# Two heads at a time: alternating the halves of the TensorE array in a block's attention matmuls

## The chip, the cores and the metric

The kernel runs on one core of a Trainium2 chip. The time is device microseconds of one execution, and the figure compared is the median of several executions.

## The reference

Two transformer blocks run one after the other on 256 tokens of width 1024, all in float32. Only the first block's attention matters here. It has two kinds of heads, eight each, of width 64, over 272 positions (16 meta tokens and the input):

```python
# forgetting attention, blocks of queries
s = einsum('bhqd,bhkd->bhqk', q, k) * scale
s = s + c[:, :, start:end, None] - c[:, :, None, :end]      # c = cumsum(log f)
p = softmax(where(s_pos <= t_pos, s, -inf))
out = einsum('bhqk,bhkd->bhqd', p, v)

# stick-breaking attention
z = einsum('bhqd,bhkd->bhqk', q, k) * scale
log_keep = where(s_pos < t_pos, log_sigmoid(-z), 0)
later = cumsum(log_keep, reverse=True) - log_keep
a = where(s_pos < t_pos, exp(log_sigmoid(z) + later), 0)
out = einsum('bhqk,bhkd->bhqd', a, v)
```

The second block has, among other things, a differential attention whose eight heads each have two score matrices of width 64.

## The kernel before

**The stream of projections.** Weights come in slabs (1024 rows by 256 columns as a rule) over SyncE's queue. ScalarE rounds each half slab to a high part (L87), and VectorE subtracts it from the raw weights to give the low part (L96). TensorE multiplies tile by tile: a tile is 128 output features, eight blocks of the contraction, three matmuls each (high by high, low by high, high by low; L320, L321, L323), 24 matmuls of 258 or 272 columns. After each tile comes one call of `period`: it starts a weight split, advances the evacuations of the last tiles, advances the side tasks by one stage, and finishes the weight split. `Side.tick` takes a new task from its queue when the clock, which counts these calls, has reached a due time; the task's gap sets the next due time. So side work is written into each engine's queue between two tiles, and the order is fixed when the kernel is written.

**Attention as side tasks.** A head's query and key are features by tokens, with head h in rows 0 to 63 or 64 to 127 of chunk h // 2. `ev_q` scales the query chunk and queues two tasks, one for each head: `fox` (forgetting) with a gap of 2 calls, `sbk` (stick-breaking) with a gap of 1.5.

- `scores` (L669 to L674) takes a PSUM bank, writes the additive causal mask into it with a bfloat16 matmul by the identity (418 columns), and adds the scores of three key blocks with float32 matmuls on the head's 64 rows: 258, 144 and 16 columns.
- `fox`: the second stage takes the maximum over key blocks (L685 and the helper at L308) and an all-reduce over partitions on GpSimd (L689). Two calls later three VectorE operations and an exponential (L696) give e. The next stage multiplies by `vext` (L699 to L703), values in 64 columns and ones in the other 64, so that numerators and denominators come in one product. Then ScalarE copies both (L710, L711), and after the odd head VectorE divides (L714) and splits the result.
- `sbk`: the second stage computes the softplus on ScalarE (L724 to L726), VectorE and ScalarE again (high part at L311, low part at L312). The third adds the reversed cumulative sum with triangular matrices (L735). The fourth takes an exponential (L738) and multiplies by the values (L743, L745, L747): 64 columns of weights, all 128 rows, and the output goes to rows 0 to 63 of a bank for the even head and 64 to 127 for the odd one. After the odd head the result is split.

A float32 matmul shows as two instructions in the trace. Score and value banks, and the banks of transposed value chunks (`ev_v`, L621 to L633), come from one pool `at` of four banks; projections have four banks of their own.

**A like pattern elsewhere.** The second block's `diff` (L1156) loops over two query blocks and, inside, over the two row halves c of the same chunk, with the outputs in two banks.

Of the kernel before, what the change touches and what calls it, by code (L numbers as in the profile page):

```python
# [11 lines left out]
F32R = mybir.dt.float32r  # L12
BF16 = mybir.dt.bfloat16
AF = mybir.ActivationFunctionType
ALU = mybir.AluOpType
# [3 lines left out]
P = 128  # L19
# [30 lines left out]
class Weights:  # L50
    """Streams weight slabs: DMA, then an exact split into two float32r parts."""

# [68 lines left out]
class Side:  # L121
    """Advances evacuations and queued side tasks by one stage per call."""

# [46 lines left out]
def two_blocks_kernel(  # L170
# [64 lines left out]

# [1 line left out]
    tab = cp.tile([P, 256], F32, name="tab")  # L237
# [52 lines left out]

# [1 line left out]
    def bank(pool, tag):  # L292
        return pool.tile([P, 512], F32, tag=tag, name=tag)

    def at():
        return bank(atp, "at")
# [4 lines left out]
    def mul(o, a, b):  # L301
        V.tensor_tensor(o, a, b, ALU.mult)  # L302
# [4 lines left out]
    def stt(o, a, s, b, op0=ALU.mult, op1=ALU.mult):  # L307
        V.scalar_tensor_tensor(out=o, in0=a, scalar=s, in1=b, op0=op0, op1=op1)  # L308
# [65 lines left out]
    class Sums:  # L374
        """Sums of squares over features, with tokens on the partitions."""

# [41 lines left out]
    def tp_tile(tag, n):  # L418
        if tag == "acc":
            return tp.tile([P, NQ], F32, tag="acc", name="acc", bufs=2)[:, :n]  # L420
        if n <= L1:
            return tp.tile([P, L1], F32, tag="s", name=tag, bufs=8)[:, :n]
        return tp.tile([P, 418], F32, tag="b", name=tag, bufs=7)[:, :n]
# [79 lines left out]

# [1 line left out]
    R = cp.tile([P, KD, NQ], F32, name="R")  # L505
# [101 lines left out]

# [1 line left out]
    u4 = unit("u4", shape=(P, KD, L1))  # L609
# [50 lines left out]
    def ev_q(q, task, gap):  # L660
        def go(ps, c):
            mul(q[:, c, :], ps[:, :NQ], rb8)
            side.add(task(2 * c), gap)
            side.add(task(2 * c + 1), gap)
            yield
        return go

    def scores(S, m, k, q, c, r):
        T.matmul(S[:, 0:418], identb, maskb[:, m, :], start=True, stop=False, skip_group_check=True)  # L669
        k, q = k[r:r + 64, c, :], q[r:r + 64, c, :]  # L670
        T.matmul(S[:, 0:258], k[:, 0:128], q, start=False, stop=False, skip_group_check=True)  # L671
        T.matmul(S[:, 258:402], k[:, 128:256], q[:, 114:258], start=False, stop=False,
                 skip_group_check=True)
        T.matmul(S[0:16, 402:418], k[:, 256:272], q[:, 242:258], start=False, stop=True,  # L674
                 skip_group_check=True)

    pair = {}

    def fox(h):
        c, r = h // 2, 64 * (h % 2)  # L680
        S = at()
        scores(S, 0, ka, qa, c, r)
        yield
        m = tp_tile("m", NQ)
        V.tensor_scalar(out=m, in0=S[:, 0:258], scalar1=ccol[:, 0, h:h + 1], scalar2=None, op0=ALU.add)  # L685
        stt(m[:, 114:258], S[:, 258:402], ccol[:, 1, h:h + 1], m[:, 114:258], ALU.add, ALU.max)
        stt(m[:, 242:258], S[:, 402:418], ccol[:, 2, h:h + 1], m[:, 242:258], ALU.add, ALU.max)
        mx = tp_tile("mx", NQ)
        G.partition_all_reduce(mx, m, P, bass_isa.ReduceOp.max)  # L689
        yield  # L690
        yield
        e = tp_tile("e", 418)
        stt(e[:, 0:258], S[:, 0:258], ccol[:, 0, h:h + 1], mx, ALU.add, ALU.subtract)
        stt(e[:, 258:402], S[:, 258:402], ccol[:, 1, h:h + 1], mx[:, 114:258], ALU.add, ALU.subtract)
        stt(e[:, 402:418], S[:, 402:418], ccol[:, 2, h:h + 1], mx[:, 242:258], ALU.add, ALU.subtract)
        A.activation(e, e, AF.Exp)  # L696
        yield
        ps = at()
        T.matmul(ps[:, 0:258], vext[:, 0, h, :], e[:, 0:258], start=True, stop=False,  # L699
                 skip_group_check=True)  # L700
        T.matmul(ps[:, 114:258], vext[:, 1, h, :], e[:, 258:402], start=False, stop=False,
                 skip_group_check=True)
        T.matmul(ps[:, 242:258], vext2[:, h, :], e[0:16, 402:418], start=False, stop=True,  # L703
                 skip_group_check=True)
        yield
        if r == 0:
            pair["o"] = tp_tile("po", NQ)
            pair["d"] = tp_tile("pd", NQ)
        po, pd = pair["o"], pair["d"]
        A.activation(po[r:r + 64], ps[r:r + 64, :NQ], AF.Copy)  # L710
        A.activation(pd[r:r + 64], ps[64 - r:128 - r, :NQ], AF.Copy)  # L711
        if r:
            yield
            V.reciprocal(pd, pd)  # L714
            mul(po, po, pd)
            split(Oh[:, c, :], Ol[:, c, :], po)

    def sbk(h):
        c, r = h // 2, 64 * (h % 2)
        S = at()  # L720
        scores(S, 1, kb, qb, c, r)
        yield
        a = tp_tile("e", 418)
        A.activation(a, S[:, 0:418], AF.Abs)  # L724
        A.activation(a, a, AF.Exp, scale=-1.0)
        A.activation(a, a, AF.Ln, bias=1.0)  # L726
        stt(a, S[:, 0:418], 0.0, a, ALU.max, ALU.add)
        ah, al = [tp.tile([P, 418], F32R, tag="b", name="sp", bufs=7) for _ in range(2)]
        split(ah, al, a)
        yield  # L730
        for o, l, i in ((S[:, 0:418], trir, ah), (S[:, 0:418], trir, al),
                        (S[:, 114:258], nones, a[:, 258:402]),
                        (S[:, 128:416].rearrange("p (a c) -> p a c", a=2)[:, :, 114:130], nones,
                         a[:, None, 402:418].to_broadcast([P, 2, 16]))):
            T.matmul(o, l, i, start=False, stop=True, skip_group_check=True)  # L735
        yield
        e = tp_tile("p", 418)
        A.activation(e, S[:, 0:418], AF.Exp)  # L738
        if r == 0:
            pair["s"] = at()  # L740
        ps = pair["s"]
        hs = slice(h * 64, h * 64 + 64)
        T.matmul(ps[r:r + 64, 0:258], vb[:, 0, hs], e[:, 0:258], start=True, stop=False,  # L743
                 skip_group_check=True)
        T.matmul(ps[r:r + 64, 114:258], vb[:, 1, hs], e[:, 258:402], start=False, stop=False,  # L745
                 skip_group_check=True)
        T.matmul(ps[r:r + 64, 242:258], vb2[:, hs], e[0:16, 402:418], start=False, stop=True,  # L747
                 skip_group_check=True)
        if r:
            yield  # L750
            split(Oh[:, 4 + c, :], Ol[:, 4 + c, :], ps[:, 0:258])

# [40 lines left out]
    for i in (0, 2):  # L793
        linear(feat_tiles(1, X1, 0, L1), KD, at_offset(ev_k(ka), i))
        linear(feat_tiles(1, X1, T0, NQ), KD, at_offset(ev_q(qa, fox, 2.0), i))
    linear(feat_tiles(2, X1, 0, L1), KD, ev_k(kb))
    linear(feat_tiles(2, X1, T0, NQ), KD, ev_q(qb, sbk, 1.5))
    linear(feat_tiles(2, X1, 0, L1), KD, lambda ps, c: ev_v(ps, c, False))
# [20 lines left out]

# [1 line left out]
    def ev_fox(ps, j):  # L821
# [54 lines left out]
    def residual(sums, after, toks, off, n, gout, gnext, fill):  # L876
        """The next linear's input from a normed residual: a maker of one chunk at a time."""
        side.evac()
# [54 lines left out]
    def ple_filler(W, stages):  # L933
        """Spreads the embedding's products over a residual's waits: one bank at a time."""
        held = []

        def fill(stage):
            if stage == 3:
                dst, src = held.pop(0)
                A.activation(dst, src, AF.Copy)  # L940
                return
            for t, c in stages[stage]:
                ps = at() if len(held) < 3 else mm()
                ts, cs = slice(t * P, (t + 1) * P), slice(c, c + 512)
                for k in range(2):
                    mm3(ps, ph[:, k, ts], pl[:, k, ts], W[0][:, k, cs], W[1][:, k, cs], k == 0, k == 1)
                held.append((ple[:, t, cs], ps))
        return fill

    box = {}  # L950

# [1 line left out]
    s1 = Sums(TOKQ, acc=True, mixed=True)  # L953
# [76 lines left out]

# [1 line left out]
    hi = unit("xh", F32R, (P, KD, L1))  # L1032
# [289 lines left out]

# [1 line left out]
    def ev_brd(ps, j):  # L1324
# [44 lines left out]

# [1 line left out]
    gh = [unit(f"u{i}", F32R) for i in (0, 1, 2, 4)]  # L1371
# [37 lines left out]

# [1 line left out]
    gfin = unit("u0", shape=(P, D))  # L1411
# [90 lines left out]
```

## Time and profile before

| | |
|---|---|
| median of 3 runs | 951.78 us (950.01 to 952.24) |
| span of the profiled execution | 950.2 us (the page gives no time around it) |
| TensorE busy | 923.9 us, 97% of the span |
| VectorE busy | 648.3 us, 68% |
| ScalarE busy | 523.5 us, 55% |
| GpSimd busy | 91.5 us, 10% |
| chain that ended last | TensorE 79%, VectorE 15%, issue 2%, ScalarE 2%, DMA 1% |

The span goes from the first to the last instruction of one execution. Busy times of one engine are the union of its instructions. Matmuls are pipelined, so their durations overlap; what one costs is read from its start to the next start.

### The profile page before, as it was taken

The numbers are of one execution on the slowest core, as the hardware profiler recorded it, in microseconds if no ns is written. First come the engines' busy times: TensorE is split into PE (matmuls) and PEld (weight loads), VectorE is DVE, ScalarE is ACT, GpSimd is POOL, SyncE is SP. The second block draws the span as 40 slices with busy tenths as digits, with TensorE's granted clock in tenths as the row PEclk, the third lists the DMA queues.
The fourth block names the chain that finished last, engine by engine and source line by source line (L and its number), as shares of the span: only waits on it lengthen the run. The fifth ranks groups of instructions, "written<-read, shape, count | busy, mean of one in ns | idle before, by whom it ended". The sixth has DMA issues, their size and how long they took to land.

```text
span 950.2 us, 18312 instructions
## 1 busy us (share of the span) xinstructions
PE 923.9 (97%) x7457; PEld 894.6 (94%) x7457; DVE 648.3 (68%) x1150; ACT 523.5 (55%) x948; POOL 91.5 (10%) x75
## 2 busy tenths in 40 slices
PE   7999999999999999899899999999999999999996
PEld 5999988999899999899899999999999999999996
DVE  4667664577699999734767774577787666655546
ACT  5534565466576666545656665445555565544435
POOL 4022100022332222001300000000000000000000
PEclk7999999999999999899999999999999999999998
DMA  8554434456255565565265556455475566565531
GB/s 263 156 156 122 121 90 111 133 180 210 89 156 178 178 179 178 167 208 179 90 202 157 152 170 192 139 165 170 136 225 173 177 200 185 177 209 179 187 130 45
DMA packets 149715, 154.73 MB, mean 163 GB/s; under 512 B 5260, under 2 KB 145808, under 8 KB 149632
## 3 DMA queue, kind: packets, MB, share of 16 engines
q1 hardware_dynamic: 147904, 149.56, 52.4%
q0 software_dynamic: 1376, 3.36, 1.1%
q8 instruction: 58, 0.95, 0.4%
q10 hardware_dynamic: 352, 0.66, 0.2%
q14 instruction: 25, 0.20, 0.1%
HBM read 152.50 MB, written 1.05 MB: 162 GB/s over the span
## 4 chain that ended last, share of the span: by engine, by line
PE 79%; DVE 15%; issue 2%; ACT 2%; DMA 1%; POOL 0%; SPq 0%; DVEq 0%; ACTq 0%
PE mm L320 20%; PE mm L323 19%; PE mm L321 19%; DVE cv L308 5%; DVE wlo L96 4%; PE mm L336 4%; PE mm L334 4%; PE mm L333 4%; DVE ur L302 2%; PE at L671 1%; DVE cv L302 1%; DMA raw<-in_w_in_dram 1%; PE at L735 1%; PE at L1156 1%; DVE u L981 1%
## 5 line engine op out<-in xcount | busy, mean ns | idle before, releaser
L87 ACT ACTIVATE whi<-raw 128x1024 fp32r<-128x1024 f32 (+1 forms) x284 | 292.3, 1047 | 186.5 <-PE mm L323 90.9
L96 DVE TENSOR_TENSOR wlo<-raw,whi 128x1024 fp32r<-128x1024 f32 (+1 forms) x267 | 325.0, 1225 | 100.1 <-ACT whi L87 99.8
L323 PE MATMUL mm<-xl,whi 128*128 128x258 f32 (+2 forms) x1256 | 351.4, 283 | 1.3 <-DVE xl L308 1.3
L320 PE MATMUL mm<-xh,whi 128*128 128x258 f32 (+3 forms) x1192 | 342.8, 288 | 3.4 <-ACT xh L542 3.4
L321 PE MATMUL mm<-xh,wlo 128*128 128x258 f32 (+3 forms) x1192 | 337.5, 284 | 0.3 <-DVE wlo L96 0.3
L323 PEld LDWEIGHTS mm<-xl,whi 128*128 128x128 f32 x1256 | 235.8, 189 | 2.0 <-DVE xl L308 1.7
L320 PEld LDWEIGHTS mm<-xh,whi 128*128 128x128 f32 (+1 forms) x1192 | 225.1, 189 | 7.0 <-ACT xh L542 3.4
L321 PEld LDWEIGHTS mm<-xh,wlo 128*128 128x128 f32 (+1 forms) x1192 | 225.2, 189 | 1.6 <-DVE wlo L96 1.2
L320 PE MATMUL mm<-u,whi 128*128 128x256 f32 (+1 forms) x704 | 198.4, 282 | 0.0
L321 PE MATMUL mm<-u,wlo 128*128 128x256 f32 (+1 forms) x704 | 197.1, 280 | 0.0
L323 PE MATMUL mm<-u,whi 128*128 128x256 f32 (+1 forms) x576 | 162.6, 282 | 0.0
L321 PEld LDWEIGHTS mm<-u,wlo 128*128 128x128 f32 x704 | 133.1, 189 | 0.0
L320 PEld LDWEIGHTS mm<-u,whi 128*128 128x128 f32 x704 | 132.5, 188 | 0.0
L323 PEld LDWEIGHTS mm<-u,whi 128*128 128x128 f32 x576 | 108.4, 188 | 0.0
L333 PE MATMUL mm<-whi,u 128*128 128x256 f32 x240 | 68.7, 286 | 2.4 <-ACT whi L87 2.4
L334 PE MATMUL mm<-wlo,u 128*128 128x256 f32 x240 | 68.9, 287 | 1.5 <-DVE wlo L96 0.9
L336 PE MATMUL mm<-whi,u 128*128 128x256 f32 x240 | 68.6, 286 | 0.0
L308 DVE SCALAR_TENSOR_TENSOR cv<-ur,gc,cv 128x256 f32<-128x256 f32 x88 | 66.3, 756 | 1.6
L96 POOL TENSOR_TENSOR wlo<-raw,whi 128x1024 fp32r<-128x1024 f32 x17 | 40.8, 2405 | 176.1 <-ACT whi L87 94.2
L302 DVE TENSOR_TENSOR u<-mm,rb 128x256 f32<-128x256 f32 (+2 forms) x68 | 28.9, 425 | 40.1 <-PE mm L323 40.1
L333 PEld LDWEIGHTS mm<-whi,u 128*128 128x128 f32 x240 | 46.4, 193 | 2.6 <-ACT whi L87 2.6
L334 PEld LDWEIGHTS mm<-wlo,u 128*128 128x128 f32 x240 | 46.6, 194 | 1.9 <-DVE wlo L96 1.1
(343 smaller groups left out, 1088.4 us busy)
## 6 DMA issues: line engine op xcount, KB each, us to landing
raw<-in_w_in_dram SPq DMA_DIRECT2D x102, 512.0 KB, 3.8
raw<-in_w_ff_dram SPq DMA_DIRECT2D x64, 512.0 KB, 3.9
raw<-in_w_up_dram SPq DMA_DIRECT2D x44, 512.0 KB, 3.6
raw<-in_w_out_dram SPq DMA_DIRECT2D x16, 512.0 KB, 4.4
raw<-in_w_down_dram SPq DMA_DIRECT2D x16, 512.0 KB, 4.8
raw<-in_w_branch_diff_dram SPq DMA_DIRECT2D x8, 512.0 KB, 3.5
raw<-in_w_branch_ret_dram SPq DMA_DIRECT2D x8, 512.0 KB, 3.4
raw<-in_w_ple_gate_dram SPq DMA_DIRECT2D x8, 512.0 KB, 3.8
```

Source lines behind the costliest of these rows:

```text
L87: self.nc.scalar.activation(hi[:, a:b], w, AF.Copy)
L96: eng.tensor_tensor(lo, w, f32(hi), ALU.subtract)
L302: V.tensor_tensor(o, a, b, ALU.mult)
L308: V.scalar_tensor_tensor(out=o, in0=a, scalar=s, in1=b, op0=op0, op1=op1)
L320: T.matmul(ps, sh, mh, start=first, stop=False)
L321: T.matmul(ps, sl, mh, start=False, stop=False)
L323: T.matmul(ps, sh, ml, start=False, stop=last)
L333: T.matmul(ps[:, 0:256], hi, W[0][:, k, :], start=first, stop=False)
L334: T.matmul(ps[:, 0:256], hi, W[1][:, k, :], start=False, stop=False)
L336: T.matmul(ps[:, 0:256], lo, W[0][:, k, :], start=False, stop=last)
L671: T.matmul(S[:, 0:258], k[:, 0:128], q, start=False, stop=False, skip_group_check=True)
L735: T.matmul(o, l, i, start=False, stop=True, skip_group_check=True)
```

## The change

The side tasks take a chunk (two heads) instead of a head. `scores` writes two masks, and then alternates the rows for each key block. `sbk` multiplies the values of both heads in alternation, into the two row halves of one bank. The gaps are doubled. The work of the other engines is written for both heads in one stage. Lines that only repeat the old stages for two heads are left out here.

```diff
     def ev_q(q, task, gap):
         def go(ps, c):
             mul(q[:, c, :], ps[:, :NQ], rb8)
-            side.add(task(2 * c), gap)
-            side.add(task(2 * c + 1), gap)
+            side.add(task(c), gap)
             yield
...
-    def scores(S, m, k, q, c, r):
-        T.matmul(S[:, 0:418], identb, maskb[:, m, :], start=True, stop=False, skip_group_check=True)
-        k, q = k[r:r + 64, c, :], q[r:r + 64, c, :]
-        T.matmul(S[:, 0:258], k[:, 0:128], q, start=False, stop=False, skip_group_check=True)
-        T.matmul(S[:, 258:402], k[:, 128:256], q[:, 114:258], start=False, stop=False,
-                 skip_group_check=True)
-        T.matmul(S[0:16, 402:418], k[:, 256:272], q[:, 242:258], start=False, stop=True,
-                 skip_group_check=True)
+    ROWS = (slice(0, 64), slice(64, 128))
+    def scores(S, m, k, q, c):
+        for i in range(2):
+            T.matmul(S[i][:, 0:418], identb, maskb[:, m, :], start=True, stop=False,
+                     skip_group_check=True)
+        for o, kk, qq in ((slice(0, 258), slice(0, 128), slice(0, 258)),
+                          (slice(258, 402), slice(128, 256), slice(114, 258)),
+                          (slice(402, 418), slice(256, 272), slice(242, 258))):
+            for i, r in enumerate(ROWS):
+                T.matmul(S[i][0:kk.stop - kk.start, o], k[r, c, kk], q[r, c, qq], start=False,
+                         stop=kk.stop == 272, skip_group_check=True)
...
+    def sbk(c):
+        S = [at(), at()]
+        scores(S, 1, kb, qb, c)
+        yield
+        parts = []
+        for s in S:
+            a = tp_tile("e", 418)
+            A.activation(a, s[:, 0:418], AF.Abs)
+            A.activation(a, a, AF.Exp, scale=-1.0)
+            A.activation(a, a, AF.Ln, bias=1.0)
+            stt(a, s[:, 0:418], 0.0, a, ALU.max, ALU.add)
+            ah, al = [tp.tile([P, 418], F32R, tag="b", name="sp", bufs=7) for _ in range(2)]
+            split(ah, al, a)
+            parts.append((a, ah, al))
+        yield
...
+        es = [tp_tile("p", 418) for _ in S]
+        for e, s in zip(es, S):
+            A.activation(e, s[:, 0:418], AF.Exp)
         ps = at()
...
+        for o, v, x, first in ((slice(0, 258), lambda hs: vb[:, 0, hs], lambda e: e[:, 0:258], True),
+                               (slice(114, 258), lambda hs: vb[:, 1, hs], lambda e: e[:, 258:402], False),
+                               (slice(242, 258), lambda hs: vb2[:, hs], lambda e: e[0:16, 402:418], False)):
+            for i, r in enumerate(ROWS):
+                h = 2 * c + i
+                T.matmul(ps[r, o], v(slice(h * 64, h * 64 + 64)), x(es[i]), start=first,
+                         stop=o.start == 242, skip_group_check=True)
...
-        linear(feat_tiles(1, X1, T0, NQ), KD, at_offset(ev_q(qa, fox, 2.0), i))
+        linear(feat_tiles(1, X1, T0, NQ), KD, at_offset(ev_q(qa, fox, 4.0), i))
...
-    linear(feat_tiles(2, X1, T0, NQ), KD, ev_q(qb, sbk, 1.5))
+    linear(feat_tiles(2, X1, T0, NQ), KD, ev_q(qb, sbk, 3.0))
```

## Rows read from the trace of the kernel before

**Rows 1.** The page: TensorE's busy time, and its granted clock in 40 slices.
```profile
PE 923.9 (97%) x7457; PEld 894.6 (94%) x7457; DVE 648.3 (68%) x1150; ACT 523.5 (55%) x948; POOL 91.5 (10%) x75
...
PEclk7999999999999999899999999999999999999998
```

**Rows 2.** Windows view: stretch, busy us by engine, PEclk, DMA share, GB/s.
```profile
47.80:181.00 133.20, 133.20 (x965) 120.09 (x963) 80.51 (x139) 65.75 (x109) 15.31 (x8) 1.00 0.44 122
385.00:405.00 20.00, 16.74 (x116) 16.34 (x115) 12.04 (x16) 12.06 (x19) 0.00 (x0) 0.83 0.58 189
```

**Rows 3.** Instructions of L671 and of L743: durations, first and last start, forms.
```profile
L671 PE MATMUL at<-u x32: 377/430/483, 48.1 to 167.7; 64*128 64x258 f32 x32
...
L743 PE MATMUL at<-p,u x16: 380/407/433, 129.0 to 180.4; 128*64 128x258 f32 x16
```

**Rows 4.** Timeline of TensorE, scores of one stick-breaking head: start, us, instruction.
```profile
161.73 0.34 PE L669 MATMUL at<-maskb,identb 128*128 128x418 bf16 x1
162.00 0.70 PE L671 MATMUL at<-u 64*128 64x258 f32 x2
...
162.87 0.21 PE L674 MATMUL at<-u 64*16 64x16 f32 x2
163.01 0.39 PE L320 MATMUL mm<-xh,whi 128*128 128x258 f32 x1
163.23 0.28 PE L321 MATMUL mm<-xh,wlo 128*128 128x258 f32 x1
163.35 0.28 PE L323 MATMUL mm<-xl,whi 128*128 128x258 f32 x1
```

**Rows 5.** Windows view of L1156 alone: stretch, TensorE busy (instructions in flight), PEclk.
```profile
500.50:500.53 0.03, 0.01 (x2) 1.00 0.19 68
```

**Rows 6.** Timeline of TensorE, second block, scores of one differential head.
```profile
500.52 0.93 PE L1156 MATMUL at<-u,u 64*128 64x128 f32 x8
501.37 0.39 PE L320 MATMUL mm<-xh,whi 128*128 128x256 f32 x1
```

**Rows 7.** Timeline of TensorE, values of one stick-breaking head.
```profile
159.82 0.65 PE L743 MATMUL at<-p,u 128*64 128x258 f32 x2
...
160.86 0.65 PE L735 MATMUL at<-sp,trir 128*128 128x418 f32 x2
```

**Rows 8.** Timeline of TensorE, vext matmuls of one forgetting head.
```profile
113.77 0.60 PE L699 MATMUL at<-e,u 128*128 128x258 f32 x2
...
114.86 0.35 PE L669 MATMUL at<-maskb,identb 128*128 128x418 bf16 x1
```

**Rows 9.** Timeline of VectorE, forgetting heads.
```profile
77.05 1.75 DVE L714 RECIPROCAL pd<-pd 128x258 f32<-128x258 f32 x1
...
80.16 1.22 DVE L96 TENSOR_TENSOR wlo<-raw,whi 128x1024 fp32r<-128x1024 f32 x1
...
81.64 0.90 DVE L308 SCALAR_TENSOR_TENSOR e<-at,ccol,mx 128x258 f32<-128x258 f32 x3
82.45 0.48 DVE L685 TENSOR_SCALAR m<-at,ccol 128x258 f32<-128x258 f32 x1
...
83.53 1.21 DVE L96 TENSOR_TENSOR wlo<-raw,whi 128x1024 fp32r<-128x1024 f32 x1
```

**Rows 10.** Timeline of ScalarE, one stick-breaking head's softplus.
```profile
163.12 0.52 ACT L724 ACTIVATE e<-at 128x418 f32<-128x418 f32 x1 [0.67 <-PE at L674]
163.67 0.56 ACT L725 ACTIVATE e<-e 128x418 f32<-128x418 f32 x1
...
165.47 0.55 ACT L311 ACTIVATE sp<-e 128x418 fp32r<-128x418 f32 x1 [0.66 <-DVE e L308]
166.17 1.06 ACT L87 ACTIVATE whi<-raw 128x1024 fp32r<-128x1024 f32 x1
```

**Rows 11.** Groups by line, 20 to 320 us: GpSimd's all-reduces (busy us, mean ns).
```profile
L689 POOL PARTITION_ALL_REDUCE mx<-m x8 | 15.3, 1913 | 79.4 <-DVE m L308 79.4
```

**Rows 12.** Timeline of VectorE, the same head's low part.
```profile
166.06 0.60 DVE L312 TENSOR_TENSOR sp<-e,sp 128x418 fp32r<-128x418 f32 x1 [0.62 <-ACT sp L311]
```

More of the change, by code (lines that the diff above doesn't have):

```diff
@@ L677, in two_blocks_kernel @@
[L677 to L682, printed above, removed]
-        yield
[L684 to L689, printed above, removed]
+    ROWS = (slice(0, 64), slice(64, 128))
@@ new lines, in fox @@
+    def fox(c):
+        heads = (2 * c, 2 * c + 1)
+        S = [at(), at()]
+        scores(S, 0, ka, qa, c)
+        yield
+        mx = []
+        for i, h in enumerate(heads):
+            m = tp_tile("m", NQ)
+            V.tensor_scalar(out=m, in0=S[i][:, 0:258], scalar1=ccol[:, 0, h:h + 1], scalar2=None,
+                            op0=ALU.add)
+            stt(m[:, 114:258], S[i][:, 258:402], ccol[:, 1, h:h + 1], m[:, 114:258], ALU.add, ALU.max)
+            stt(m[:, 242:258], S[i][:, 402:418], ccol[:, 2, h:h + 1], m[:, 242:258], ALU.add, ALU.max)
+            mx.append(tp_tile("mx", NQ))
+            G.partition_all_reduce(mx[i], m, P, bass_isa.ReduceOp.max)
@@ L690, in fox @@
         yield
         yield
[L692 to L696, printed above, removed]
-        yield
-        ps = at()
-        T.matmul(ps[:, 0:258], vext[:, 0, h, :], e[:, 0:258], start=True, stop=False,
-                 skip_group_check=True)
@@ L701, in fox @@
[L701 to L704, printed above, removed]
-        yield
[L706 to L751, printed above, removed]
@@ new lines, in fox @@
+        es = []
+        for i, h in enumerate(heads):
+            e = tp_tile("e", 418)
+            for k, (o, n) in enumerate(((0, 258), (258, 144), (402, 16))):
+                stt(e[:, o:o + n], S[i][:, o:o + n], ccol[:, k, h:h + 1], mx[i][:, 258 - n:258],
+                    ALU.add, ALU.subtract)
+            A.activation(e, e, AF.Exp)
+            es.append(e)
+        yield
+        ps = [at(), at()]
+        for i, h in enumerate(heads):
+            e = es[i]
+            T.matmul(ps[i][:, 0:258], vext[:, 0, h, :], e[:, 0:258], start=True, stop=False,
+                     skip_group_check=True)
+            T.matmul(ps[i][:, 114:258], vext[:, 1, h, :], e[:, 258:402], start=False, stop=False,
+                     skip_group_check=True)
+            T.matmul(ps[i][:, 242:258], vext2[:, h, :], e[0:16, 402:418], start=False, stop=True,
+                     skip_group_check=True)
@@ new lines, in fox @@
+        yield
+        po, pd = tp_tile("po", NQ), tp_tile("pd", NQ)
+        for i, r in enumerate(ROWS):
+            A.activation(po[r], ps[i][r, :NQ], AF.Copy)
+            A.activation(pd[r], ps[i][ROWS[1 - i], :NQ], AF.Copy)
+        yield
+        V.reciprocal(pd, pd)
+        mul(po, po, pd)
+        split(Oh[:, c, :], Ol[:, c, :], po)
+    def sbk(c):
+        S = [at(), at()]
+        scores(S, 1, kb, qb, c)
+        yield
+        parts = []
[8 more added lines that the diff above has]
+            parts.append((a, ah, al))
+        yield
+        for s, (a, ah, al) in zip(S, parts):
+            for o, l, i in ((s[:, 0:418], trir, ah), (s[:, 0:418], trir, al),
+                            (s[:, 114:258], nones, a[:, 258:402]),
+                            (s[:, 128:416].rearrange("p (a c) -> p a c", a=2)[:, :, 114:130], nones,
+                             a[:, None, 402:418].to_broadcast([P, 2, 16]))):
+                T.matmul(o, l, i, start=False, stop=True, skip_group_check=True)
+        yield
+        es = [tp_tile("p", 418) for _ in S]
+        for e, s in zip(es, S):
+            A.activation(e, s[:, 0:418], AF.Exp)
+        ps = at()
+        for o, v, x, first in ((slice(0, 258), lambda hs: vb[:, 0, hs], lambda e: e[:, 0:258], True),
+                               (slice(114, 258), lambda hs: vb[:, 1, hs], lambda e: e[:, 258:402], False),
+                               (slice(242, 258), lambda hs: vb2[:, hs], lambda e: e[0:16, 402:418], False)):
+            for i, r in enumerate(ROWS):
+                h = 2 * c + i
+                T.matmul(ps[r, o], v(slice(h * 64, h * 64 + 64)), x(es[i]), start=first,
+                         stop=o.start == 242, skip_group_check=True)
+        yield
+        split(Oh[:, 4 + c, :], Ol[:, 4 + c, :], ps[:, 0:258])
```

## The prediction

> **What bounds the kernel now.** I read the page first: TensorE is busy 97% of the span, and its granted clock is full in nearly all of the 40 slices [rows 1]. The windows view says the same of the stretch of the first block's attention: from 47.8 to 181.0 us TensorE is busy 133.20 of 133.20 us at a clock of 1.00, VectorE 80.5 and ScalarE 65.8 us [rows 2]. So in this stretch what TensorE spends is what the kernel spends, and the other engines matter only if they make it wait. The count of the two lines that the change regroups says how often they come: 32 half-matmuls of L671 between 48.1 and 167.7 us (16 heads, two instructions for each float32 matmul) and 16 of L743 (8 heads) [rows 3]. I then read start to start in the order of time, because the busy times of pipelined matmuls overlap.
>
> **Scores, before.** One head's scores run from the mask matmul at 161.73 to the next projection matmul at 163.01: 1.28 us, of which 0.27 goes from the mask's start to the first 64-row matmul (418 columns at the pace of the projections, 258 in 0.12, would be 0.19; the rest is the change from 128 rows to 64) and 1.01 to the six half-matmuls on 64 rows [rows 4]. The first projection matmul after them takes 0.22 to the next start where a later one takes 0.12: 0.10 for going back [rows 4]. So a head costs 1.28 + 0.10 = 1.38 us, sixteen heads 22.1 us.
>
> **Scores, after.** A pair issues two masks, then 258, 144 and 16 columns, each for rows 0 to 63 and at once for rows 64 to 127, into two different banks. Does this overlap? The second block's differential attention already does it: L1156 issues 128 and 256 columns for two row halves into two banks. In a window of 0.03 us around 500.52 two of its matmuls have started [rows 5], and its eight halves take 0.85 us (500.52 to 501.37) [rows 6]: that is two heads in the time in which here one head's 258 and 144 columns take 0.87 (162.00 to 162.87) [rows 4]. So I take the second half as free. A pair then costs 0.19 (first mask) + 1.28 + 0.10 = 1.57 us against 2.76: 1.19 less, **9.5 us** over eight pairs. Bounds: a second mask that costs the full 0.27 takes back 0.08 x 8 = 0.6; no overlap at all leaves only the saved changes of rows, 0.27 - 0.19 + 0.10 = 0.18 a pair, 1.4 us.
>
> **Stick-breaking values.** One head's value matmuls (L743, L745, L747; 64 columns of weights, all rows) run from 159.82 to 160.86: 1.04 us, eight heads 8.3 us [rows 7]. After, the halves alternate between column halves 0 to 63 and 64 to 127 of one bank, each with its own 128-row moving operand. No row here shows two column halves in flight together. Bounds: full overlap gives 4 x 1.04 = 4.2 us; one after the other gives 0; if each of the five hand-overs in a pair costs the 0.10 that a change of rows costs, 2.0 us are lost. I take 4.2, because the nearest row is the other kind of half on the same array, and that overlaps within 0.03 us.
> The Trainium skill, on the page "TensorE: Matmul & The Clock Gate", section "Packing small matmuls — row/col tiling", says that a weight load overlaps matmuls in flight only when the row group differs; column halves share all row groups. By that rule the value term would be 0 and the sum 9.5 instead of 13.7. No run here shows column halves side by side; the same section also lists a speedup for column tiles.
>
> **What stays beside.** The vext matmuls of the forgetting heads (1.09 us a head, 113.77 to 114.86 [rows 8]) and the triangular ones are the same instructions, now two heads at one call, and I cost them at nothing. ScalarE, VectorE and GpSimd do the same operations, but two heads in one call of the side queue, every four (forgetting) or three (stick-breaking) calls instead of two or one and a half. So the question is whether TensorE now waits.
> Forgetting heads: in four calls TensorE has four tiles of 24 matmuls at 0.12 = 11.5, two heads' vext matmuls 2.2 and a pair's scores 1.5: 15.2 us. VectorE has four times a product and a low split (1.48), one reciprocal group (77.05 to 80.16, 3.11), two times e (0.81) and two times m (1.08) [rows 9]: 12.8 us. In order: m can start when the scores are done, 3.8 us after the call; both m end at 6.0; split and product 7.4; the previous pair's reciprocal group 10.6; split and product 12.0; e of the first head 12.9, of the second 13.7. With an exponential of 0.56 [rows 10] the values are ready at 13.4 and 14.2, and TensorE asks for them at 15.2 and 16.3. Hidden, by 1.8 us. The two all-reduces of 1.9 us on GpSimd [rows 11] run one behind the other from 4.9 to 8.7, before e needs them; nothing else stands in that queue.
> Stick-breaking heads: one head's chain goes from the absolute value at 163.12 to the end of the high split at 166.02 on ScalarE [rows 10] and to 166.66 on VectorE [rows 12]. The second head follows on ScalarE 2.90 later, so the last low part is ready 2.90 + 3.54 = 6.4 us after the scores. TensorE comes back after two tiles, 5.8 us, works 0.9 us on the first head's triangular matmuls (160.86 to 161.73 [rows 4, 7]), and wants the second head's low part at about 6.8. Hidden, by 0.4 us only. What is queued behind on ScalarE is the weight split of the following call (1.06 us [rows 10]), whose slab TensorE needs about two tiles later.
> Banks: at one call the last forgetting pair holds two, a transposed value chunk one, and the first stick-breaking pair asks for two, five of a pool of four. The last waits for ScalarE's two copies of the chunk, behind one split of 1.06; 2.2 us of vext matmuls cover it. Uncovered it would cost some 2 us, once. SyncE's weight loads keep their order and follow TensorE; no DMA is added or moved.
>
> **Sum.** 9.5 + 4.2 = 13.7 us. The profiled execution's span is 950.2, so its own span would be 936.5. The page gives no time around the span; the runs (950.01 to 952.24) leave under 2 us for it, and their median 951.78 stands 1.6 above the span. Against the median: 951.8 - 13.7 = **938.1**.
>
> **Rivals.**
> *Only the row halves overlap* (scores gain, values don't). For: no row shows column halves together, and two full 128-row operands would have to stream at once, which the row halves don't ask for. Against: nothing in the rows either. 951.8 - 9.5 = 942.3, up to 944.3 with the hand-overs. The rule of the Trainium skill cited above would make it this case.
> *The pair's chain is late.* For: the stick-breaking margin is 0.4 us; one weight split on ScalarE (1.06) and its low part on VectorE (1.22 [rows 9]) between the two heads make TensorE wait 1.9 us in each of four pairs: 938.1 + 7.5 = 945.6. Against: the splits are issued ahead of the pair in each call, and ScalarE reaches them while TensorE still does the scores.
> *Slower than before.* The same wait at L735, with two splits and two low parts in the chain (4.6 us): 4.2 x 4 = 16.7 us, 954.8. It decides from 13.7 / 4 = 3.4 us of wait a pair, a chain of 10.2 instead of 6.4 us. VectorE's and ScalarE's shares of 60% and 50% [rows 2] speak against it.
> *It doesn't do what it says*: the score halves don't overlap, say because they add to a bank that the mask has just filled, which L1156 does not. Then 1.4 us are left: 950.4.
>
> **How the numbers follow.** Forecast 0.55, only rows 0.26, late chain 0.12, no overlap 0.04, slower 0.03. About 0.3%, 2.9 us, is what a measurement of this kernel can tell from no change. Faster by more than that: the first three, 0.93; within it: 0.04; slower: 0.03. The range 934.5 to 944.3 holds the first two cases with their bounds, 0.81. Its lower end also has the clock: from 385 to 405 us the granted clock is 0.83 [rows 2], so 6.8 of 20 us run at 1.2 GHz instead of 2.4, after TensorE was idle 3.3 us in that window; everything there comes some 14 us earlier, and if the slow piece doesn't come, half of it, 3.4 us, is gained.
>
> **What would show it.** Right: the row halves start in pairs some 0.01 us apart; a pair's scores take about 1.5 us from the first mask to the next projection matmul; L743 to L747 take 1.04 us for two heads; TensorE has no idle time in the stretch, which ends 13 to 14 us earlier. Wrong: 2.1 us for a pair's values (then 942.3); TensorE idle in front of L735 or L699, released by ScalarE or VectorE (late chain); scores of 2.6 us a pair (no overlap).

## The result, and the profile after

| | before | after |
|---|---|---|
| median | 951.92 us (950.01 to 952.24, 4 runs) | 937.26 us (936.75 to 937.62, 4 runs) |
| span of the profiled execution | 950.2 us | 935.8 us |
| first mask matmul to first output projection | 142.1 us | 129.7 us |

The ratio is 0.9848, with a 95% interval of 0.9836 to 0.986: 1.5% faster. The forecast was 938.1. In the runs shown here an execution's time is some 1.8 us above its span (937.62 for the profiled one, with a span of 935.8), which the page of the kernel before did not tell.

The page after, the rows that answer to [rows 1]:
```profile
PE 909.7 (97%) x7457; PEld 884.8 (95%) x7457; DVE 647.0 (69%) x1150; ACT 522.5 (56%) x948; POOL 88.1 (9%) x75
...
PEclk8999999999999999999999999999999999999998
```
TensorE runs the same 7457 matmuls and is busy 14.2 us less; the other engines have what they had. (GpSimd's 3.4 us less is in its all-reduces, which now come two at a time: the trace shows the first of a pair as 1.1 us instead of 1.9.)

For the stretch itself I take two points that both kernels have: the first mask matmul, and the first matmul of the output projections behind the attention. The windows view of that stretch, first of the kernel before and then of the changed one (stretch, busy us by engine in the order PE, PEld, DVE, ACT, POOL, then the clock):
```profile
47.83:189.91 142.08, 142.08 (x1039) 128.97 (x1037) 85.27 (x144) 70.06 (x114) 15.31 (x8) 1.00 0.44 123
```
```profile
45.97:175.64 129.67, 128.59 (x1038) 119.79 (x1037) 84.66 (x144) 69.11 (x114) 11.93 (x8) 1.00 0.46 134
```
The stretch is 12.4 us shorter at a full clock. Before, TensorE was never idle in it; now it is for 1.08 us. The span fell by 14.4: 12.4 here, and 1.9 because the stretch begins at 45.97 and not at 47.83, though nothing ahead of it was changed. That part is told apart below.

One call of the side queue after, in the timeline of TensorE; the rows that answer to [rows 4] and [rows 7], now for two heads:
```profile
136.68 0.28 PE L323 MATMUL mm<-xl,whi 128*128 128x258 f32 x1
136.89 0.90 PE L756 MATMUL at<-p,u 128*64 128x258 f32 x8
137.73 0.29 PE L756 MATMUL at<-p,ple 16*64 16x16 f32 x4
137.95 0.53 PE L672 MATMUL at<-maskb,identb 128*128 128x418 bf16 x2
138.41 1.10 PE L678 MATMUL at<-u 64*128 64x258 f32 x12
139.44 0.39 PE L320 MATMUL mm<-xh,whi 128*128 128x258 f32 x1
139.66 0.28 PE L321 MATMUL mm<-xh,wlo 128*128 128x258 f32 x1
```
Values of two heads: 136.89 to 137.95, 1.06 us, where one head took 1.04. Scores of two heads with both masks: 137.95 to 139.44, 1.49 us, where one head took 1.28. The windows view of L678 (row halves) and of L756 (column halves), cut to 0.03 us around a start, has two matmuls in flight in each case. The last line is the same view of the column halves in the run of the first experiment below, which has one half after the other and shows one:
```profile
138.40:138.43 0.03, 0.02 (x2) 1.00 0.86 307
...
136.88:136.91 0.03, 0.02 (x2) 1.00 0.64 205
...
136.45:136.48 0.03, 0.02 (x1) 1.00 0.45 137
```
So the two in flight are the two halves, and both kinds run side by side. And the one idle piece, in the view of who waited for whom (engine and line waited for: us, times, longest):
```profile
PE at L756 <- ACT p L749: 1.1, 1, 1.1
```

### The profile page after: what moved, and what is told of

Its sections match the earlier page's. It is cut to its first block, busy times and chain, and to the rows that moved or that the text cites. A ratio compares the mean times of both kernels' runs of the same rounds, so it can differ in the third digit from the quotient of the medians.

```text
span 935.8 us, 18318 instructions
## 1 busy us (share of the span) xinstructions
PE 909.7 (97%) x7457; PEld 884.8 (95%) x7457; DVE 647.0 (69%) x1150; ACT 522.5 (56%) x948; POOL 88.1 (9%) x75
## 4 chain that ended last, share of the span: by engine, by line
PE 77%; DVE 16%; ACT 3%; issue 2%; DMA 1%; POOL 0%; SPq 0%; DVEq 0%; ACTq 0%
PE mm L320 19%; PE mm L323 19%; PE mm L321 19%; DVE cv L308 5%; DVE wlo L96 4%; PE mm L336 4%; PE mm L333 4%; PE mm L334 4%; DVE ur L302 2%; DVE cv L302 1%; PE at L678 1%; DMA raw<-in_w_in_dram 1%; PE at L1164 1%; ACT whi L87 1%; DVE u L989 1%
```

## The experiments

Each figure below called "the stretch" goes from the first mask matmul to the first output projection of that run's trace. Single executions carry some 2 us of chance, as the control shows, and the medians a part of it (those of the changed kernel differ by 1.1); the stretch carries none of it, except where a piece at 1.2 GHz falls into it, as with the longer chain.

**Values one after the other.** The two loops of the value matmuls change places:
```diff
-        for o, v, x, first in (...):
-            for i, r in enumerate(ROWS):
+        for i, r in enumerate(ROWS):
+            for o, v, x, first in (...):
```


> The changed kernel with the value matmuls of a stick-breaking pair one head after the other; the scores still alternate. Theory (both kinds of halves overlap): the values of a pair cost 2.1 us instead of the 1.05 that the changed kernel's trace shows, four pairs, so 4 us slower than the changed kernel: about 941.4. Rival (column halves do not overlap, and the gain came from elsewhere): as the changed kernel, 937.3 within 1 us.

Measured: 941.94 us, ratio to the kernel before on the same chip 0.99 (0.9874 to 0.9926); the stretch 133.36. The values of a pair in the timeline:
```profile
136.46 0.90 PE L756 MATMUL at<-p,u 128*64 128x258 f32 x4
...
137.50 0.90 PE L756 MATMUL at<-p,u 128*64 128x258 f32 x4
...
138.54 0.53 PE L672 MATMUL at<-maskb,identb 128*128 128x418 bf16 x2
```
2.08 us (136.46 to 138.54) against 1.06 for the same instructions in alternation. The stretch is 3.7 us longer than the changed kernel's; column halves overlap, and their order in the queue is what makes them. Four pairs at 1.02 would be 4.1; the missing 0.4 is in the first pair, whose second head waits in the changed kernel (its values take 1.44 us, 123.46 to 124.90; below).

**Scores one after the other.** The same exchange in `scores`, the values left in alternation:
```diff
-        for o, kk, qq in (...):
-            for i, r in enumerate(ROWS):
+        for i, r in enumerate(ROWS):
+            for o, kk, qq in (...):
```


> The changed kernel with the six 64-row score matmuls of a pair one head after the other; the values still alternate. Theory: the second head's six half-matmuls cost their 1.0 us again, less a little overlap where one head ends and the other begins, eight pairs: 8 us slower than the changed kernel, about 945.2. Rival (the gain lies in regrouping the work by pairs, whatever the order of the matmuls): as the changed kernel, 937.3 within 1 us.

Measured: 945.93 us, ratio 0.9932 (0.991 to 0.9955); the stretch 136.62, 7.0 us longer than the changed kernel's. The scores of the first pair:
```profile
46.83 0.53 PE L672 MATMUL at<-maskb,identb 128*128 128x418 bf16 x2
47.29 2.10 PE L678 MATMUL at<-u 64*128 64x258 f32 x12
49.32 0.39 PE L320 MATMUL mm<-xh,whi 128*128 128x272 f32 x1
```
The same twelve half-matmuls take 2.03 us from start to next start where the alternating ones take 1.03. Eight pairs at 1.0 are 8.0. Of these 1.1 do not show: in this trace TensorE is idle for only 0.07 us at the first stick-breaking pair's values, since with more to do it comes there later.

**Pairs alone.** Both exchanges at once.

> Pairs of heads in one side task as in the changed kernel, but no alternation in scores or values. Theory: the two terms add, 8 + 4 = 12 us slower than the changed kernel, about 949.3; what is left against the kernel before (2.6 us) is fewer changes between 128 and 64 rows, less the 1.1 us wait for the first pair's exponentials, and what the clock does at the start. Rival (regrouping is what gained): well under 945.

Measured: 947.9 us, ratio 0.9964 (0.9948 to 0.9979); the stretch 140.30, 10.6 longer than the changed kernel's and 1.8 shorter than before. So the regrouping gains 1.8 us by itself; alternating the scores takes it from 140.30 to 133.36 (6.9), alternating the values from there to 129.67 (3.7). In the other order it is 3.7 for the values (140.30 to 136.62) and 7.0 for the scores. The two add up. (The median is 4.2 below the kernel before; what exceeds 1.8 lies outside the stretch.)

**The kernel before, again.** No edit.

> The kernel before, unchanged, profiled again. Both its profile and the changed kernel's run the same instructions up to the first scores, yet these begin at 47.8 and 46.0 us, and the half-speed stretch of the clock at the start is 10.2 and 6.8 us long. If that is the chance of an execution, this profile can have either, and the difference of 1.9 us is no part of the change; if the kernel before always starts late, it begins again at 47.8.

Measured: the stretch 142.05, the span 950.4. The windows view of 230 to 250 us in this execution, and under it in the first one of the same kernel:
```profile
230.00:250.00 20.00, 18.40 (x109) 16.55 (x109) 13.54 (x26) 8.65 (x23) 6.55 (x7) 0.83 0.41 124
```
```profile
230.00:250.00 20.00, 18.23 (x132) 16.65 (x132) 15.31 (x27) 10.42 (x26) 6.54 (x7) 1.00 0.44 133
```
The stretch begins at 46.05 this time, as in the changed kernel, and not at 47.83. Instead TensorE's clock falls to 1.2 GHz from 238.5 to 245.3 us (0.83 over 20 us), where the first execution kept 2.4 GHz with nearly the same idle time of TensorE (1.6 us here, 1.8 there). Twelve traces stand behind this study. Four have such a piece between 223 and 246 us, of the kernel before and of variants of the changed one alike, and there the time from the output projections to the end is 762.3 to 762.6 us, in the other eight 759.9 to 760.3. So the 1.9 us at the start and the 2.3 us there differ between executions of one kernel. The first is no part of the change, whose instructions come later. Of the second that is not shown: the piece is in one of two traces of the kernel before, in none of three of the changed kernel and in three of seven of its variants, too few to say that the change has no part in how often it comes.

**The changed kernel, again.** No edit.

> The changed kernel, unchanged, profiled and timed again. From the first mask to the first output projection its trace showed 129.67 us, and two traces of the kernel before 142.07 and 142.05; this one should show 129.7 within 0.1, 12.4 less than before. If the medians again differ by more than 12.4, the rest lies outside this stretch, in how long TensorE runs at half speed in an execution.

Measured: 938.04 us, ratio 0.9862 (0.9845 to 0.988), the stretch 129.65. A third time, beside the last experiment: 938.35, ratio 0.9867 (0.9843 to 0.9891), the stretch 129.66. The stretch repeats to 0.02 us; the medians are 14.7, 13.7 and 13.6 below the kernel before, each in its own comparison.

**The split one call later.** One `yield` in `fox`:
```diff
         V.reciprocal(pd, pd)
         mul(po, po, pd)
+        yield
         split(Oh[:, c, :], Ol[:, c, :], po)
```


> The changed kernel with the split of a forgetting pair's result one call later than its division. Theory (TensorE waits 1.1 us, and 0.4 more between the first two value matmuls, because ScalarE stands in front of the exponentials of the first stick-breaking pair until VectorE has divided the last forgetting pair): the wait goes, and the stretch from the first mask to the first output projection falls from 129.67 to 128.2 to 128.6 us. Rival (the exponentials are late because the two heads' softplus chains are late): the wait stays and the stretch is 129.7.

Measured: the stretch 128.35, 1.3 us less; the median 937.74 (ratio 0.9854, 0.9835 to 0.9873) can't tell it from the changed kernel. The four executions have a mean granted clock of 0.987, where the changed kernel's beside them have 0.989, and the profiled one shows a piece at half speed from 223.4 to 230.3 us. The waits view shows no wait, but the first pair's values still take 1.26 us instead of 1.06: 0.2 of the 0.4 between their halves are left. What ScalarE does ahead of the exponentials (L749) in the changed kernel:
```profile
121.22 0.42 ACT L311 ACTIVATE u<-po 128x258 fp32r<-128x258 f32 x1 [2.90 <-DVE po L302]
121.54 1.04 ACT L87 ACTIVATE whi<-raw 128x1024 fp32r<-128x1024 f32 x1
122.49 0.36 ACT L632 ACTIVATE u<-at 128x256 f32<-128x256 f32 x1
122.75 0.25 ACT L633 ACTIVATE ple<-at 16x128 f32<-16x128 f32 x1
122.91 0.89 ACT L749 ACTIVATE p<-at 128x418 f32<-128x418 f32 x2
```
and with the late split:
```profile
117.69 1.04 ACT L87 ACTIVATE whi<-raw 128x1024 fp32r<-128x1024 f32 x1
118.64 0.36 ACT L632 ACTIVATE u<-at 128x256 f32<-128x256 f32 x1
118.91 0.25 ACT L633 ACTIVATE ple<-at 16x128 f32<-16x128 f32 x1
120.69 0.42 ACT L311 ACTIVATE u<-po 128x258 fp32r<-128x258 f32 x1 [1.53 <-DVE po L302]
121.01 0.91 ACT L750 ACTIVATE p<-at 128x418 f32<-128x418 f32 x2
```
In the changed kernel ScalarE stands idle for 2.90 us in front of the high split of the last forgetting pair, until VectorE has divided, and a weight split and the copies of a value chunk then lie between it and the exponentials. With the split one call later these two go ahead of that idle time (1.53 us there), and the exponentials follow the high split directly. The softplus chains were not late; the rival falls.

**A longer chain.** One copy more in the softplus:
```diff
             A.activation(a, a, AF.Ln, bias=1.0)
+            A.activation(a, a, AF.Copy)
```


> The changed kernel with one more copy of 418 columns on ScalarE in each stick-breaking head's softplus, after the logarithm, 0.58 us each and 1.17 for a pair; it changes nothing in the values. Theory (the second head's low part is ready some 0.4 us before TensorE wants it): TensorE waits in front of or between the triangular matmuls for about 0.7 us in the later three pairs, and the first pair's exponentials come 1.2 us later still, so the stretch is 2.5 to 3.5 us longer than 129.67. Rival (the chain has ample room): the stretch is within 0.3 us of 129.67.

Measured: 944.95 us, ratio 0.9934 (0.9919 to 0.9949); the stretch 135.54, 5.9 us longer. The waits of TensorE:
```profile
PE at L757 <- ACT p L750: 2.0, 1, 2.0
PE at L746 <- ACT sp L311: 0.5, 2, 0.3
PE at L746 <- DVE sp L312: 0.4, 2, 0.2
```
The windows view behind the first of them:
```profile
125.00:134.00 9.00, 8.97 (x52) 7.24 (x52) 3.23 (x6) 5.59 (x11) 0.00 (x0) 0.62 0.39 117
```
Matched start by start with the changed kernel's trace, each counted from its own first mask, TensorE falls behind by 0.2 us at the first pair's triangular matmuls, by 1.0 in front of the first values, by 2.9 while the clock is low behind that wait (0.62 over 9 us: 6.8 us ran at 1.2 GHz), and by 0.9 in each of the last two pairs: 5.9. Without the clock it is 3.0, in the middle of what was expected. In the second pair, whose scores ran at half speed, there is no delay; 0.7 in each of three pairs was expected.

The waits view gives only 0.4 us for each of the last two pairs, since it counts only time in which no matmul is in flight. From start to start one of them costs twice that. The triangular matmuls of the third pair, up to the next projection matmul, in the changed kernel and with the longer chain:
```profile
145.28 0.54 PE L745 MATMUL at<-sp,trir 128*128 128x418 f32 x2
...
146.90 0.37 PE L320 MATMUL mm<-xh,whi 128*128 128x258 f32 x1
```
```profile
149.79 0.54 PE L746 MATMUL at<-sp,trir 128*128 128x418 f32 x2
...
150.97 0.45 PE L746 MATMUL at<-sp,trir 128*128 128x418 f32 x1 [0.25 <-ACT sp L311]
151.60 0.46 PE L746 MATMUL at<-sp,trir 128*128 128x418 f32 x1 [0.18 <-DVE sp L312]
...
152.28 0.37 PE L320 MATMUL mm<-xh,whi 128*128 128x258 f32 x1
```
1.62 us become 2.49. A chain that is 1.17 us longer and costs 0.87 had about 0.3 us of room. The changed kernel's own trace shows it too: VectorE ends the second head's low part at 145.88, and TensorE begins the matmul that reads it at 146.32, 0.44 later (timelines of the two engines):
```profile
145.28 0.60 DVE L312 TENSOR_TENSOR sp<-e,sp 128x418 fp32r<-128x418 f32 x1 [0.62 <-ACT sp L311]
146.32 0.35 PE L745 MATMUL at<-sp,trir 128*128 128x418 f32 x1
```
So the forecast's 0.4 us of room stands. Ample room, the rival, it is not.

**Sixteen rows together.** With the late split; the 16-row `vext` matmuls of both heads go behind the others:
```diff
         for i, h in enumerate(heads):
-            e = es[i]
             T.matmul(ps[i][:, 0:258], vext[:, 0, h, :], ...)
             T.matmul(ps[i][:, 114:258], vext[:, 1, h, :], ...)
-            T.matmul(ps[i][:, 242:258], vext2[:, h, :], ...)
+        for i, h in enumerate(heads):
+            T.matmul(ps[i][:, 242:258], vext2[:, h, :], ...)
```


> The late split of the run before, and the 16-row vext matmuls of a forgetting pair together behind the 258 and 144 column ones of both heads. Theory (each passage from 128 rows to 16 and back costs 0.1 us or so, and a pair then makes one instead of two): 0.1 us a pair, 0.4 to 0.6 us less than with the late split alone. Rival (the passages cost nothing): as with the late split alone.

Measured: 935.64 us, ratio 0.9838 (0.982 to 0.9857); the stretch 127.18, 1.2 us less than with the late split alone, where 0.4 to 0.6 was expected. One pair's vext matmuls, first in the changed kernel, then grouped:
```profile
59.36 0.60 PE L709 MATMUL at<-e,u 128*128 128x258 f32 x2
59.79 0.41 PE L711 MATMUL at<-e,u 128*128 128x144 f32 x2
60.13 0.39 PE L713 MATMUL at<-e,u 16*128 16x16 f32 x2
60.45 0.70 PE L709 MATMUL at<-e,u 128*128 128x258 f32 x2
60.99 0.41 PE L711 MATMUL at<-e,u 128*128 128x144 f32 x2
...
61.65 0.53 PE L672 MATMUL at<-maskb,identb 128*128 128x418 bf16 x2
```
```profile
60.01 0.60 PE L708 MATMUL at<-e,u 128*128 128x258 f32 x2
60.44 0.41 PE L710 MATMUL at<-e,u 128*128 128x144 f32 x2
60.69 0.60 PE L708 MATMUL at<-e,u 128*128 128x258 f32 x2
61.12 0.41 PE L710 MATMUL at<-e,u 128*128 128x144 f32 x2
61.46 0.61 PE L713 MATMUL at<-e,u 16*128 16x16 f32 x4
62.01 0.53 PE L672 MATMUL at<-maskb,identb 128*128 128x418 bf16 x2
```
2.29 us becomes 2.00. A 144-column step takes 0.34 to the next start in front of 16-row matmuls and 0.25 in front of 128-row ones; the 258-column step behind 16 rows takes 0.54, otherwise 0.43; the rest is in the 16-row matmuls. A passage to 16 rows and back costs 0.29, not 0.1; four pairs at 0.29 are the 1.2.

The same kernel again, beside the changed one:

> The kernel with the late split and the grouped 16-row matmuls, once more, beside the changed kernel on the same chip. Its trace had 127.18 us from the first mask to the first output projection, 2.5 less than the changed kernel's 129.65; the medians should differ by about that, within 1.5 us for what the clock does outside the stretch. If they are equal, what the stretch gained is given back later.

> The changed kernel, for the comparison: the stretch at 129.7 us, the median between 937 and 938.5.

Measured: 934.78 us against 938.35, 3.6 apart; the stretch 127.18 again against 129.66. Ratios to the kernel before 0.9834 (0.9809 to 0.9858) and 0.9867 (0.9843 to 0.9891). The intervals overlap, so the medians by themselves don't settle it. The stretch does, twice, by 2.5 us. This is the fastest version of the study, 16 to 17 us under the kernel before.

## Why the prediction was right

**The scores.** "A pair then costs 1.57 us against 2.76" stands: 1.49 from the first mask to the next projection matmul and 0.10 for going back, 1.59. The second mask costs little: twelve half-matmuls begin 0.46 us after the first mask (137.95 to 138.41 above), 0.19 more than the 0.27 behind a single one, as the forecast had it. Reading L1156 in the second block was enough; the row halves start in pairs here too. (The last rival, score halves that don't overlap, drops the values' 4.2 us as well without a reason: with 1.4 and 4.2 gained it stands at 946.2, not at 950.4.)

**The values.** Taken at 4.2 with bounds of 4.2 and -2.0. They came out at 1.02 a pair, 4.1, and the experiment with the exchanged loops shows that it is the overlap of column halves. The rule of the Trainium skill (page "TensorE: Matmul & The Clock Gate", section "Packing small matmuls — row/col tiling") that loads pass matmuls only where the row group differs would have made this term 0; the prediction left out that the same section also lets a load pass that goes into the background weight buffer. Here halves in the same four row groups have both matmuls in flight, four of their weight loads run meanwhile, and by the order alone 2.08 us become 1.06. The measurement decides. The windows view of L756 (TensorE busy, then weight loads):
```profile
136.94:137.09 0.15, 0.15 (x2) 0.15 (x4) 1.00 1.22 198
```
The kernel before had told against the plain rule too: in [rows 2] weight loads are busy for 120.09 of 133.20 us in which TensorE never stops multiplying, mostly on all 128 rows. For column tiles the same section of the Trainium skill lists a speedup of 2.38 with three of them; here two give 2.08 / 1.06, 1.96.

**The regrouping.** The forecast had 1.4 us for fewer passages in the scores; the run with pairs alone gained 1.8. I had left out the passage into the values, once a pair instead of once a head: a projection matmul in front of L743 or L756 takes 0.21 to the next start instead of 0.12 (136.68 to 136.89 above), four times 0.09. The two make 1.8, but that is not all of it (below, with the sum).

**The waits.** Right for the forgetting heads (no wait at L709) and for the triangular matmuls (none at L745; the room of 0.4 us is what the trace has, though the sum's own figures, 5.8 + 0.9 - 6.4, give 0.3). The step that failed is "hidden" for everything behind those two, and with it the sign "TensorE has no idle time in the stretch": I followed each kind of head in its own steady rhythm, and the fifth bank at the passage between them, but not ScalarE's order there. The last forgetting pair's division and split stand ahead of the first stick-breaking pair's exponentials, and cost 1.1 us in front of the values and 0.4 between their halves; the late split took back 1.3. No wait shows at the scores that ask for the fifth bank. The price of this wait is like that of the rival of the late chain, at another line and once instead of four times.

**The sum.** 9.4 + 4.1 + 0.35 - 1.5 = 12.4, the stretch's 12.4; the forecast said 13.7. That it fits to the tenth is in part luck, since two small terms are not in it. The vext matmuls, which the prediction cost at nothing, take 2.29 us for a pair where two heads took 2 x 1.09: the second head's first matmul now stands behind 16-row ones, 0.11 a pair, 0.4 in all. Start to start over the whole stretch, triangular matmuls and transposes take 0.3 less. The median fell by 14.7, 13.7 and 13.6 in three comparisons; the 1 to 2 us above 12.4 lie outside the stretch, where the control shows the clock's chance to be of that size. All three came out above, so that chance is the whole of it is not shown. That the forecast of 938.1 hit 937.26 within 0.9 us is in part this luck: 951.8 less the stretch's 12.4 is 939.4. The clock term at the lower end of the range (3.4 us, which gives 934.7 and not 934.5) did not come: in place of the one piece of 6.8 us at half speed near 391 us the changed kernel has two of 3.4, at 377.7 and 449.4.

## What to carry to other kernels

Where a kernel has matmuls on 64 rows or 64 columns for many independent heads, order the queue so that neighbours use different halves: here that alone, with the same instructions, took half of their time away, and a like loop elsewhere in the same trace had told so in advance. Writing two heads into one stage makes the other engines' chains twice as long, so follow each in-order engine through the passage from one kind of task to the next, not only through the steady rhythm. And compare a fixed stretch of the trace, not only medians: the stretch repeated to 0.02 us where medians moved by 1. Read a wait's price from start to start as well: the waits view showed half of it.

## What was not expected of the hardware

Two column halves in float32, each with its own moving operand on all 128 rows, cost 0.02 us more than one (1.06 against 1.04). A passage between 128-row and 16-row matmuls and back costs 0.29 us, where one between 128 and 64 rows and back costs 0.18 (0.08 and 0.10, from [rows 4]). A wait of TensorE of 2.0 us was followed by 6.8 us at 1.2 GHz, in which it fell 2.9 us behind; in the changed kernel a wait of 1.1 us at the same place was not, in three traces.
